# Log-sum-exp of 16,384 rows: an empty operation with a wait on VectorE, one wait for the last logarithms, and another list of loads

## The chip, the core and the metric

The kernel runs on one NeuronCore of a Trainium2 chip. The metric is the device time of one execution in microseconds (us); the median of three runs of the kernel before is 162.41 us (162.29 to 162.56). The profile is of one further execution.

## What is computed

For `x` of shape 32 x 512 x 1024 in float32, the logarithm of the sum of exponentials of each row of 1024:

```
max_x = np.max(x, axis=-1, keepdims=True)
max_x.squeeze(-1) + np.log(np.sum(np.exp(x - max_x), axis=-1))
```

The kernel takes the exponentials without subtracting the maximum, sums and takes the logarithm; at the end it tests that all sums lie in a safe range, and only if one does not, a second, slow pass with the maximum follows (it is in the program behind a branch, and isn't executed with this data).

## The kernel before

The 16,384 rows are spread over the 128 partitions, 128 rows of 1024 columns to each: 131,072 columns of a partition, 512 bytes of HBM for each column over all partitions, 67.1 MB in all. Nineteen loads (load 0 to load 18, list `LOADS`, L20) bring them into a ring of 48 rows in SBUF. The first number of an entry is the size of the load in rows; sizes are not whole rows, so a load may end inside one. They fall from 16 rows (16,384 columns) to 480 and 448 columns.

SyncE issues all loads in order (`load`, L130, the DMA itself L136). It waits only where a load overwrites a part of the ring that is still to be read: the helper `Counted.wait` puts a wait for the reader's count in front. Each load has a semaphore of its own.

ScalarE takes the exponential of each load in place, in one or several ACTIVATEs (L224), each with one wait for the load. The string of an entry says how the rows that are then whole are summed:

- `R8`: VectorE reduces eight rows in one TENSOR_REDUCE (L235).
- `G4`: GpSimd adds the right half of four rows to the left (L230), and a later `H` has VectorE reduce the halves (L154).
- `T3`: three times for one row, VectorE adds the right half to the left and sums the result into one number in the same instruction (`add_halves`, L159; L162 in the profile). The profile shows behind each a second instruction, the read of the accumulator. Such a pair is called a T below.
- `a` and `b`: the last row comes in two loads. `a` is exponentiated and summed by a shorter T (288 columns a half); `b` is summed by ScalarE itself in its ACTIVATE (L219), followed by a read of its accumulator.
- `C`: VectorE works out the least and the total of the sums found so far (L171), for the test.
- `L`: ScalarE takes the logarithms of the first 112 rows early (L197), and SyncE stores them (L255).

The last part, behind the loop over the loads, is this: ScalarE waits until VectorE has summed all rows but the last, takes 15 logarithms (L259), waits for VectorE's sum of `a` and for its own sum of `b`, and takes the last logarithm of their sum (L262). SyncE stores the 16 results (L266). Beside this VectorE tests the remaining sums (L270, L274), TensorE adds the flags up over the partitions (L279 to L282), VectorE compares (L286), ScalarE and VectorE read the flag and branch, and SyncE clears the semaphores and waits for the store.

The order on each engine is the order of the code; there is no scheduler. The waits that matter for the change: VectorE waits before the first T of each load for ScalarE's exponential of that load (`dve.wait(act, at)`); where an instruction has one such wait it carries it itself.

Of the kernel before, what the change touches and what calls it, by code (L numbers as in the profile page):

```python
# [10 lines left out]
RING = 48  # L11
B = 16

# [1 line left out]


LOADS = [  # L20
# [5 lines left out]
]  # L26


# [23 lines left out]
def kernel(  # L52
# [5 lines left out]
    nc = tc.nc  # L58
# [15 lines left out]
    H = d // 2  # L74
    W = NC - B
    LAST = NC - 1
# [36 lines left out]
    act = Counted(nc, nc.scalar, "act")  # L113
    dve = Counted(nc, nc.vector, "dve")
# [15 lines left out]
    def load(i, here, done_before, size):  # L130
        for a, b, who, at in users:
            if a < here + size and b > here:
                sp.wait(who, at)
        assert not any(p0 < here + size and p0 + s * d > here for _, p0, s, _ in folded)
        users[:] = [u for u in users if not (u[0] < here + size and u[1] > here)]
        return nc.sync.dma_start(  # L136
            out=ring[:, here : here + size], in_=source(done_before, size)
        ).then_inc(landed[i], 16)
# [7 lines left out]
    summed = []  # L146
# [3 lines left out]
    def sum_folded():  # L150
        for c0, p0, s, at in folded:
            dve.wait(pool, at)
            half = ring[:, p0 : p0 + s * d].rearrange("p (c d) -> p c d", d=d)[:, :, 0:H]
            at = dve.did(nc.vector.reduce_sum(out=sumexp[:, c0 : c0 + s], in_=half, axis=AX.X))  # L154
            users.append((p0, p0 + s * d, dve, at))
            summed.append((c0, c0 + s, at))
        folded.clear()

    def add_halves(v, col):  # L159
        h = v.shape[-1] // 2  # L160
        lo = v[:, 0:h]
        return dve.did(nc.vector.scalar_tensor_tensor(  # L162
            out=lo, in0=lo, scalar=1.0, in1=v[:, h : 2 * h],
            op0=ALU.mult, op1=ALU.add, accum_out=sumexp[:, col : col + 1],
        ))

    def check_early(c):
        dve.wait(act, summed_by_act)
        dve.wait(dve, dve.n)
        for op, col in ((ALU.min, LEAST), (ALU.add, TOTAL)):  # L170
            dve.did(nc.vector.tensor_reduce(  # L171
                out=sumexp[:, col : col + 1], in_=sumexp[:, 0:c], op=op, axis=AX.X
            ))

    for i, (size, parts) in enumerate(loads):
        if here + size > RING * d:
            assert here == p
            p = here = 0
        dma = load(i, here, done_before, size)
        first_load = first_load or dma.ins  # L180
        end = here + size
        done_before += size
        act.wait(landed[i], 16)
        for k, part in enumerate(parts):
            if part[0][0] == "H":
                sum_folded()
                continue
            if part[0][0] == "C":
                assert not folded
                checked = c  # L190
                check_early(c)
                continue
            if part[0][0] == "L":
                assert c >= W
                assert dve.seen[act.sem.num] >= summed_by_act
                act.wait(dve, max(at for c0, _, at in summed if c0 < W))
                ln_early = act.did(nc.scalar.activation(  # L197
                    out=res[:, 0:W], in_=sumexp[:, 0:W], func=AF.Ln
                ))
                continue  # L200
            if part[0][0] == "A":
                assert here == p
                for _ in range(part[0][1]):
                    v = ring[:, p : p + d]
                    summed_by_act = act.did(nc.scalar.activation(
                        out=v, in_=v, func=AF.Exp, accum_out=sumexp[:, c : c + 1]
                    ))
                    users.append((p, p + d, act, summed_by_act))
                    by_act += 1
                    c += 1  # L210
                    p += d
                    here += d
                continue
            rows = sum(s for how, s in part if how in "RTG")
            more = any(q[0][0] not in "HLC" for q in parts[k + 1 :])
            upto = p + rows * d if more else end
            v = ring[:, here:upto]
            if part[-1][0] == "b":
                last = act.did(nc.scalar.activation(  # L219
                    out=v, in_=v, func=AF.Exp, accum_out=sumexp[:, REST : REST + 1]  # L220
                ))
                here = upto
                continue
            at = act.did(nc.scalar.activation(out=v, in_=v, func=AF.Exp))  # L224
            here = upto
            for how, s in part:
                rows = ring[:, p : p + s * d].rearrange("p (c d) -> p c d", d=d)
                if how == "G":
                    pool.wait(act, at)
                    folded.append((c, p, s, pool.did(nc.gpsimd.tensor_tensor(  # L230
                        out=rows[:, :, 0:H], in0=rows[:, :, 0:H], in1=rows[:, :, H:d], op=ALU.add,
                    ))))
                elif how == "R":
                    dve.wait(act, at)
                    users.append((p, p + s * d, dve, dve.did(nc.vector.reduce_sum(  # L235
                        out=sumexp[:, c : c + s], in_=rows, axis=AX.X
                    ))))
                    summed.append((c, c + s, dve.n))
                elif how == "T":
                    dve.wait(act, at)  # L240
                    for r in range(s):
                        n_sums = add_halves(rows[:, r, :], c + r)
                        users.append((p + r * d, p + (r + 1) * d, dve, n_sums))
                        summed.append((c + r, c + r + 1, n_sums))
                elif how == "a":
                    dve.wait(act, at)
                    summed.append((LAST, NC, add_halves(ring[:, p:upto], LAST)))
                    s = 0
                c += s
                p += s * d  # L250
        assert here == end
# [3 lines left out]
    nc.sync.dma_start(out=out_rows, in_=res[:, 0:W]).then_inc(sp.sem, 16)  # L255

    sums = dve.n
    act.wait(dve, max(at for c0, _, at in summed if c0 < LAST))
    act.did(nc.scalar.activation(out=res[:, W:LAST], in_=sumexp[:, W:LAST], func=AF.Ln))  # L259
    act.wait(dve, sums)  # L260
    act.wait(act, last)
    ln_last = act.did(nc.scalar.activation(  # L262
        out=res[:, LAST:NC], in_=sumexp[:, REST : REST + 1], func=AF.Ln, bias=sumexp[:, LAST:NC]
# [10 lines left out]
    at = dve.did(nc.vector.reduce_sum(  # L274
        out=total, in_=sumexp[:, checked : TOTAL + 1], axis=AX.X
    ))
# [5 lines left out]
    at = pe.did(nc.tensor.matmul(  # L282
        count, lhsT=ones, rhs=sumexp[:, REST : REST + 1], start=False, stop=True
    ))
    dve.wait(pe, at)
    at = dve.did(nc.vector.tensor_scalar(out=fine, in0=count, scalar1=HIGH, scalar2=None, op0=ALU.is_lt))  # L286
# [111 lines left out]
```

## Time and profile before

| | us |
|---|---|
| median of three runs | 162.41 |
| profiled execution, its own time | 162.43 |
| its span, from the first to the last instruction | 161.1 |
| busy: VectorE, ScalarE, GpSimd, TensorE | 111.2, 114.7, 44.4, 0.3 |

The span is 1.3 us shorter than the time of the same execution; that part lies around the program. Times in the rows count from the start of the span. In a row of the timeline stand the start, the duration, the engine, the line, the operation, what it writes and reads, how often, and in brackets the idle time before it and who ended it. Lines `L...` are those of the kernel before.

### The profile page before, as it was taken

To read this page: it belongs to the slowest core of one execution; us is meant where nothing else is said; L and a number is where in the kernel's file an instruction comes from. 1 tells how busy PE (TensorE), PEld (TensorE's weight loads), DVE (VectorE), ACT (ScalarE), POOL (GpSimd) and SP (SyncE) were. 2 spreads that over 40 slices of the span, in tenths; PEclk is the share of its full clock that TensorE was granted. 3 is DMA by queue.
4 is the path that set the end of the run, shared out by engine and by line. 5 is a ranking of instruction groups with operands and counts; after the bars stand their busy time and mean duration, and the time that the engine had idled before them with its cause. 6 is when DMAs were issued, how large, how long until landed. Compare 5 with 4: busy or idle time off the path is not lost.

```text
span 161.1 us, 185 instructions
## 1 busy us (share of the span) xinstructions
PE 0.3 (0%) x6; PEld 0.2 (0%) x6; DVE 111.2 (69%) x57; ACT 114.7 (71%) x30; POOL 44.4 (28%) x16
## 2 busy tenths in 40 slices
PE   0000000000000000000000000000000000000000
PEld 0000000000000000000000000000000000000000
DVE  0000000009999699959997299988939999999995
ACT  3000059990899529990599719997994999999995
POOL 0000000000000000008409992005009579895000
DMA  8996996999799799969997999989899999999991
GB/s 277 505 521 277 505 511 287 479 511 411 343 498 498 343 408 504 504 268 488 485 485 318 409 432 461 485 378 469 383 479 403 394 410 443 427 412 428 417 402 30
DMA packets 3025, 67.18 MB, mean 417 GB/s; under 512 B 592, under 2 KB 848, under 8 KB 1488
## 3 DMA queue, kind: packets, MB, share of 16 engines
q1 hardware_dynamic: 3024, 67.18, 97.4%
q14 instruction: 1, 0.01, 0.0%
HBM read 67.11 MB, written 0.07 MB: 417 GB/s over the span
## 4 chain that ended last, share of the span: by engine, by line
DMA 56%; ACT 23%; DVE 13%; another core or an unknown queue 3%; SPq 2%; issue 0%; PE 0%
DMA ring<-in_x_dram 56%; ACT ring L224 23%; DVE sumexp L235 13%; SPq L136 2%; DVE ring L162 0%; DVE clamped L270 0%; PE count L279 0%; DVE fine L286 0%; DVE total L274 0%; PE count L282 0%; PE count L280 0%
## 5 line engine op out<-in xcount | busy, mean ns | idle before, releaser
L224 ACT ACTIVATE ring<-ring 128x3072 f32<-128x3072 f32 (+22 forms) x24 | 112.3, 4730 | 43.5 <-DMA ring<-in_x_dram 43.4
L235 DVE TENSOR_REDUCE sumexp<-ring 128x3 f32<-128x3072 f32 (+7 forms) x9 | 79.2, 8803 | 47.8 <-ACT ring L224 47.8
L230 POOL TENSOR_TENSOR ring<-ring 128x2048 f32<-128x2048 f32 (+4 forms) x10 | 44.1, 4420 | 101.4 <-ACT ring L224 101.4
L154 DVE TENSOR_REDUCE sumexp<-ring 128x4 f32<-128x2048 f32 (+4 forms) x10 | 22.1, 2224 | 0.1
L162 DVE SCALAR_TENSOR_TENSOR ring<-ring 128x512 f32<-128x512 f32 (+1 forms) x16 | 9.8, 671 | 0.6 <-ACT ring L224 0.4
L123 ACT ACT_TABLE_LOAD x1 | 1.3, 1283 | 1.4 <-PEq L61 1.4
L162 DVE DVE_READ_ACCUMULATOR ring<-ring 128x1 f32 x16 | 1.3, 81 | 0.0
L219 ACT ACTIVATE ring<-ring 128x448 f32<-128x448 f32 x1 | 0.6, 559 | 0.0
L279 PE MATMUL count<-far,bad 128*1 128x1 f32 x2 | 0.2, 163 | 159.6 <-DVE total L274 159.6
L286 DVE TENSOR_SCALAR fine<-count 1x1 int32<-1x1 f32 x1 | 0.1, 147 | 0.5 <-PE count L282 0.5
L171 DVE TENSOR_REDUCE sumexp<-sumexp 128x1 f32<-128x89 f32 x2 | 0.4, 240 | 0.0
L124 POOL MEMSET ones<- 128x1 f32 x1 | 0.1, 99 | 1.0 <-POOLq L61 1.0
L279 PEld LDWEIGHTS count<-far,bad 128*1 128x1 f32 x2 | 0.1, 80 | 159.6 <-issue 159.6
L262 ACT ACTIVATE res<-sumexp 128x1 f32<-128x1 f32 x1 | 0.3, 294 | 0.0
L197 ACT ACTIVATE res<-sumexp 128x112 f32<-128x112 f32 x1 | 0.3, 279 | 0.0
L270 DVE SCALAR_TENSOR_TENSOR clamped<-sumexp 128x40 f32<-128x40 f32 x1 | 0.2, 200 | 0.0
L259 ACT ACTIVATE res<-sumexp 128x15 f32<-128x15 f32 x1 | 0.2, 197 | 0.0
L274 DVE TENSOR_REDUCE total<-sumexp 128x1 f32<-128x41 f32 x1 | 0.2, 190 | 0.0
L280 PE MATMUL count<-total,ones 128*1 128x1 f32 x2 | 0.2, 163 | 0.0
L282 PE MATMUL count<-sumexp,ones 128*1 128x1 f32 x2 | 0.2, 163 | 0.0
L219 ACT ACTIVATION_READ_ACCUMULATOR ring<-ring 128x1 f32 x1 | 0.2, 186 | 0.0
L382 POOL MEMSET const-float32-0.0<- 128x1 f32 x1 | 0.1, 99 | 0.2 <-issue 0.2
(7 smaller groups left out, 0.7 us busy)
## 6 DMA issues: line engine op xcount, KB each, us to landing
ring<-in_x_dram SPq DMA_DIRECT2D x1, 8032.0 KB, 39.5
ring<-in_x_dram SPq DMA_DIRECT2D x1, 7920.0 KB, 25.0
ring<-in_x_dram SPq DMA_DIRECT2D x1, 7840.0 KB, 57.7
ring<-in_x_dram SPq DMA_DIRECT2D x1, 7632.0 KB, 25.4
ring<-in_x_dram SPq DMA_DIRECT2D x1, 5952.0 KB, 25.5
ring<-in_x_dram SPq DMA_DIRECT2D x1, 5360.0 KB, 21.2
ring<-in_x_dram SPq DMA_DIRECT2D x1, 3968.0 KB, 24.2
ring<-in_x_dram SPq DMA_DIRECT2D x1, 2448.0 KB, 20.1
```

Source lines behind the costliest of these rows:

```text
L123: nc.scalar.preload_act_table_set("natural_log_exp_and_others")
L136: return nc.sync.dma_start(out=ring[:, here : here + size], in_=source(done_before, size)).then_inc(landed[i], 16)
L154: at = dve.did(nc.vector.reduce_sum(out=sumexp[:, c0 : c0 + s], in_=half, axis=AX.X))
L162: return dve.did(nc.vector.scalar_tensor_tensor(out=lo, in0=lo, scalar=1.0, in1=v[:, h : 2 * h], op0=ALU.mult, op1=ALU.add, accum_out=sume ...
L171: dve.did(nc.vector.tensor_reduce(out=sumexp[:, col : col + 1], in_=sumexp[:, 0:c], op=op, axis=AX.X))
L197: ln_early = act.did(nc.scalar.activation(out=res[:, 0:W], in_=sumexp[:, 0:W], func=AF.Ln))
L219: last = act.did(nc.scalar.activation(out=v, in_=v, func=AF.Exp, accum_out=sumexp[:, REST : REST + 1]))
L224: at = act.did(nc.scalar.activation(out=v, in_=v, func=AF.Exp))
L230: folded.append((c, p, s, pool.did(nc.gpsimd.tensor_tensor(out=rows[:, :, 0:H], in0=rows[:, :, 0:H], in1=rows[:, :, H:d], op=ALU.add,))))
L235: users.append((p, p + s * d, dve, dve.did(nc.vector.reduce_sum(out=sumexp[:, c : c + s], in_=rows, axis=AX.X))))
L262: ln_last = act.did(nc.scalar.activation(out=res[:, LAST:NC], in_=sumexp[:, REST : REST + 1], func=AF.Ln, bias=sumexp[:, LAST:NC]))
L279: pe.did(nc.tensor.matmul(count, lhsT=bad, rhs=far, start=True, stop=False))
```

## The change

Four edits. (1) Ahead of the T of load 15, the fourth load from the end, VectorE gets an empty operation; the wait for ScalarE's exponential of load 15, which the T carried, then stands in front of the empty operation, and in the built program it is an instruction of its own that only waits. (2) The 15 logarithms now wait for VectorE's last sum, that of `a`, and no longer for the last but one; the separate wait ahead of the last logarithm is gone. (3) Nine of the nineteen loads have other sizes, as the table shows; loads 0 to 8 and load 10 keep theirs. (4) Some entries have other strings: load 2 is reduced by VectorE alone, load 4 is cut in three ACTIVATEs and is reduced by VectorE alone, load 6 has its `C` one step later, and loads 11 and 12 have two Ts each in place of three and one.

| load | 9 | 10 | 11 | 12 | 13 | 14 | 15 | 16 | 17 `a` | 18 `b` |
|---|---|---|---|---|---|---|---|---|---|---|
| columns before | 4512 | 3232 | 2496 | 1760 | 1280 | 928 | 640 | 608 | 480 | 448 |
| columns after | 4256 | 3232 | 2528 | 1696 | 1376 | 992 | 672 | 640 | 512 | 480 |

```diff
+HELD = 15
...
-    (16, "R16"), (15.6875, "R15"), (15.3125, "R11+G5 H"), (15.46875, "G7 R3+G5 H"),
-    (14.90625, "R6 H G2+R7 H"), (11.625, "R8+G4"), (10.46875, "H C G4 H R3 G3"),
-    (7.75, "H G4 R4 H"), (4.78125, "G2 H G3 H"), (4.40625, "T4"), (3.15625, "T3 L"),
-    (2.4375, "T3"), (1.71875, "T1"), (1.25, "T1"), (0.90625, "T1"), (0.625, "T1"),
-    (0.59375, "T1"), (0.46875, "a"), (0.4375, "b"),
+    (16, "R16"), (15.6875, "R15"), (15.3125, "R16"), (15.46875, "G7 R3+G5 H"),
+    (14.90625, "R4 R7 R4"), (11.625, "R8+G4"), (10.46875, "H G4 H C R3 G3"), (7.75, "H G4 R4 H"),
+    (4.78125, "G2 H G3 H"), (4.15625, "T4"), (3.15625, "T3 L"), (2.46875, "T2"), (1.65625, "T2"),
+    (1.34375, "T1"), (0.96875, "T1"), (0.65625, "T1"), (0.625, "T1"), (0.5, "a"), (0.46875, "b"),
...
                 elif how == "T":
                     dve.wait(act, at)
+                    if i == HELD:
+                        nc.vector.nop(nofuse=True)
                     for r in range(s):
...
-    act.wait(dve, max(at for c0, _, at in summed if c0 < LAST))
+    act.wait(dve, sums)
     act.did(nc.scalar.activation(out=res[:, W:LAST], in_=sumexp[:, W:LAST], func=AF.Ln))
-    act.wait(dve, sums)
     act.wait(act, last)
```

## The prediction

> **What bounds the kernel now.** I read the page's DMA part first, then the chain of waits, then the DMA view and the table by stretches at its last step, then the timeline of the last 12 us.
>
> ```profile
> DMA packets 3025, 67.18 MB, mean 417 GB/s; under 512 B 592, under 2 KB 848, under 8 KB 1488
> ...
> q1 hardware_dynamic: 3024, 67.18, 97.4%
> q14 instruction: 1, 0.01, 0.0%
> ```
>
> The DMA engines are busy 97.4% of the span: from the first load to the last the kernel moves bytes, and only what stands behind the last bytes can be saved. One packet is no load: q14, an instruction packet.
>
> ```profile
> 132.07 0.45 SPq L136
> 132.52 0.04 issue
> 132.56 25.45 DMA ring<-in_x_dram
> 158.01 0.02 issue
> 158.03 0.61 ACT ring L224
> 158.64 0.02 issue
> 158.67 0.48 DVE ring L162 x2
> ...
> 159.50 0.14 issue
> ```
>
> The chain ends with load 17 (`a`), landed at 158.01; ScalarE's exponential, VectorE's T and the test follow without a gap over 0.14. Was `a` on time? Load 16 was issued at 132.07 and has this row (304 KB, last column us to landing):
>
> ```profile
> ring<-in_x_dram SPq DMA_DIRECT2D x1, 304.0 KB, 24.7
> ```
>
> So it landed at 156.77. Here is the table by stretches (busy time of PE, PEld, DVE, ACT, POOL, then clock, DMA share, GB/s):
>
> ```profile
> 150.00:157.00 7.00, 0.00 (x0) 0.00 (x0) 6.88 (x25) 7.00 (x8) 0.00 (x0) 1.00 1.01 410
> ```
> ```profile
> 157.50:157.95 0.45, 0.00 (x0) 0.00 (x0) 0.45 (x3) 0.00 (x0) 0.00 (x0) 1.00 0.08 22
> 157.95:158.30 0.35, 0.00 (x0) 0.00 (x0) 0.28 (x2) 0.27 (x1) 0.00 (x0) 1.00 0.05 15
> 158.30:160.40 2.10, 0.29 (x6) 0.21 (x6) 0.93 (x6) 1.28 (x5) 0.00 (x0) 1.00 0.00 0
> 160.40:160.70 0.30, 0.00 (x0) 0.00 (x0) 0.00 (x0) 0.00 (x0) 0.00 (x0) 1.00 0.31 28
> ```
>
> At 410 GB/s a column (512 bytes) takes 1.25 ns: `a` (480 columns) was due at 156.77 + 0.60 = 157.37 and `b` (448) at 157.93. `a` came 0.64 late. And from 157.50 to 158.30 the share is 0.08 and 0.05, about one engine of sixteen (0.06): a single DMA engine is behind while the others have finished. The DMA view of the stretch 156.57 to 156.58 has the cause that I take:
>
> ```profile
> q14 instruction: 1, 0.01, 193.1%
> ```
>
> This packet, 193.1% of 16 x 0.01 us = 0.31 us long, sits in one engine's queue just as `a` ends and `b` begins. It fetches instructions for some engine. So the bound at the end is one DMA engine, late by 0.64.
>
> **Whose packet.** From 156 on GpSimd, TensorE and SyncE stand in waits or are done; ScalarE and VectorE advance. VectorE goes through the most instructions there, two for each T:
>
> ```profile
> 150.39 7.10 ACT L224 ACTIVATE ring<-ring 128x2496 f32<-128x2496 f32 x6
> ...
> 155.48 0.68 DVE L162 SCALAR_TENSOR_TENSOR ring<-ring 128x512 f32<-128x512 f32 x1
> ...
> 156.29 0.69 DVE L162 SCALAR_TENSOR_TENSOR ring<-ring 128x512 f32<-128x512 f32 x1
> ...
> 156.92 0.69 DVE L162 SCALAR_TENSOR_TENSOR ring<-ring 128x512 f32<-128x512 f32 x1
> ...
> 157.54 0.69 DVE L162 SCALAR_TENSOR_TENSOR ring<-ring 128x512 f32<-128x512 f32 x1
> 158.03 0.60 ACT L224 ACTIVATE ring<-ring 128x480 f32<-128x480 f32 x1 [0.55 <-DMA ring<-in_x_dram]
> ...
> 158.54 0.56 ACT L219 ACTIVATE ring<-ring 128x448 f32<-128x448 f32 x1
> 158.67 0.46 DVE L162 SCALAR_TENSOR_TENSOR ring<-ring 128x288 f32<-128x288 f32 x1 [0.44 <-ACT ring L224]
> 159.01 0.19 ACT L219 ACTIVATION_READ_ACCUMULATOR ring<-ring 128x1 f32 x1
> 159.05 0.08 DVE L162 DVE_READ_ACCUMULATOR ring<-ring 128x1 f32 x1
> 159.10 0.20 ACT L259 ACTIVATE res<-sumexp 128x15 f32<-128x15 f32 x1
> 159.17 0.20 DVE L270 SCALAR_TENSOR_TENSOR clamped<-sumexp 128x40 f32<-128x40 f32 x1
> 159.29 0.29 ACT L262 ACTIVATE res<-sumexp 128x1 f32<-128x1 f32 x1
> ...
> 159.61 0.34 SPq L266 DMA_DIRECT2D out_dram<-res  x1
> ```
>
> The Ts of loads 13 to 16 start at 155.48, 156.29, 156.92, 157.54. From request to packet there is a lag that no row gives; the nearest is the last store, issued at 159.61 with no data before 160.40: 0.8 us. Then the fetch was asked for by 155.8, while VectorE executed load 13's T. If VectorE asked, its sequencer reads ahead of the engine, and the request came from some instruction behind. Load 14's T is the next, load 15's the one after.
>
> The Trainium skill's page "Advanced Engine Details and Errata", section "Engine Queue Depths", gives VectorE a queue of eight instructions, four Ts; by it the request would come from well behind the hold. No run here shows that depth.
>
> **The change part by part.**
>
> *The empty operation.* In the built program the number of VectorE instructions up to load 15's T is the same as before (one reduction fewer, one instruction that only waits), so the fetch belongs to the same later instruction. A wait in an instruction of its own holds the sequencer. It ends with load 15's exponential, about 156.75 (below). A request from behind it then comes after 156.8, and its packet 0.8 or more later, at 157.6 or after: behind the last bytes of the loads on that engine. Queued behind the hold are the Ts of 15, 16, `a`, and the test. Its own price: a wait in an instruction costs 0.02 (158.64 in the chain), TensorE's, in an instruction of its own, 0.14 (159.50). I take 0.10, being nearer to TensorE's; both ends are hidden, as the sum shows.
>
> *Loads 2, 4, 6.* More of it falls to VectorE:
>
> ```profile
> 72.83 11.89 DVE L235 TENSOR_REDUCE sumexp<-ring 128x11 f32<-128x11264 f32 x1 [2.06 <-ACT ring L224]
> ...
> 91.74 3.35 DVE L235 TENSOR_REDUCE sumexp<-ring 128x3 f32<-128x3072 f32 x1 [4.29 <-ACT ring L224]
> ...
> 96.23 13.02 ACT L224 ACTIVATE ring<-ring 128x5664 f32<-128x5664 f32 x2 [4.52 <-DMA ring<-in_x_dram]
> 101.53 6.54 DVE L235 TENSOR_REDUCE sumexp<-ring 128x6 f32<-128x6144 f32 x1
> ...
> 120.48 8.69 DVE L235 TENSOR_REDUCE sumexp<-ring 128x8 f32<-128x8192 f32 x1 [2.45 <-ACT ring L224]
> ...
> 139.28 4.42 DVE L235 TENSOR_REDUCE sumexp<-ring 128x4 f32<-128x4096 f32 x1 [0.37 <-ACT ring L224]
> ```
>
> Sixteen rows instead of eleven at 1.08 each: load 2's reduction ends at 90.1, under the 4.29 idle before 91.74. SyncE issues load 5 behind it, at 90.1, not 84.7; load 4 keeps the DMA busy until 96.2, so 6 us of cover remain. Load 4: R4, R7, R4 = 4.42 + 7 x 1.08 + 4.42 = 16.4 from 101.53, to 118.0, ahead of the 120.48 of load 5. The later `C` only swaps 0.4 us with a reduction. Nothing. If that cover were gone, a late load would cost its delay one for one.
>
> *The sizes.* Bytes are the same, so `b` still ends at 157.93 without the late engine. From the end backwards `b` has 480 columns, `a` 512, load 16 640: `a` lands at 157.93 - 0.60 = 157.33, load 16 at 156.69. Behind load 11 stand 224 columns more than before, so it lands 0.28 earlier and ScalarE starts it at 150.11. The six ACTIVATEs of loads 11 to 16 in the row at 150.39 take 7.10 for 7712 columns; these two rows of the groups by form give the price of a column:
>
> ```profile
> L224 ACT ACTIVATE ring<-ring 128x16384 f32<-128x16384 f32 x1 | 13.9, 13857 | 19.3 <-DMA ring<-in_x_dram 19.3
> ...
> L224 ACT ACTIVATE ring<-ring 128x480 f32<-128x480 f32 x1 | 0.6, 602 | 0.5 <-DMA ring<-in_x_dram 0.5
> ```
>
> (13857 - 602)/(16384 - 480) = 0.83 ns. With 7904 columns: 7.26, the end at 157.37; as load 16 lands only at 156.69, 157.43. Load 15's ends about 156.75, ScalarE is free again at 157.34.
>
> *The tail, without the late engine.* `a`: landed 157.33, start 157.35, 0.60 + 32 x 0.83 ns = 0.63, end 157.98. `b`: starts 157.95, its read 0.47 + 0.03 later (159.01 - 158.54), ends 158.64. VectorE: load 15's T at 156.85, a T every 0.61 to 0.62 (156.92 to 157.54), load 16's at 157.46, where its exponential (157.43) has just come, so the hold's 0.10 is hidden, and 0.14 would move it 0.03. `a`'s T follows at 158.08: VectorE, not ScalarE, binds here. Against 158.67 that is 0.59 earlier; with 16 columns fewer a half its sum is there 0.45 + 0.03 later, 158.56.
>
> *One wait.* The 15 logarithms now wait for that sum, 158.56; before they started at 159.10, ahead of VectorE's read end (159.13). Alone this costs up to 0.05. The last logarithm comes 0.19 behind (159.29 - 159.10), at 158.75 and not 159.29; the store, still 0.32 behind, at 159.07. `b`'s sum (158.64) is hidden under it. The test starts 0.60 earlier and isn't last.
>
> **Sum:** 159.07 - 159.61 = -0.54. The profiled execution took 162.43, 0.02 over the median: 161.89, or **161.9**.
>
> **Rivals.**
>
> 1. *The fetch is held too briefly.* If the lag is under 0.5, the packet comes at 157.1 to 157.5, in `b` instead of `a`. `b` is then late by up to 0.64, `a` on time, the last logarithm waits for ScalarE's sum: 162.2 to 162.45, I take 162.3. The store's 0.8 speaks against it.
>
> 2. *The fetch isn't moved*: it is ScalarE's, or its instruction lies before the hold. `a` lands 0.64 late at 157.97, starts 0.04 earlier and takes 0.03 longer; the single wait takes 0.05 back: 162.45. For it: the row names no engine. Against it: VectorE need read only two Ts ahead.
>
> The Trainium skill ("Runtime: NRT & Kernel Launch", "Instruction fetch mechanics") calls the cost of such a fetch "mostly hidden"; by that rule nothing is won here, as in rival 2. The trace disagrees: 0.64 beside a 0.31 packet.
>
> 3. *Slower: the sequencer needs the block at once.* If VectorE cannot go on until the fetched instructions are there, before its queue covered this and the hold takes the cover away. A request at 156.9, 0.8 lag, 0.31 packet and it continues at 158.0 or later, 158.5 with a lag of 1.3. If the missing instruction is load 15's T or the next to it, it and load 16's T (2 x 0.61) put `a`'s T at 159.2 to 159.7, 0.55 to 1.05 behind 158.67: 163.2. It decides only if the boundary lies ahead of load 16's T; one T further it costs under 0.3. Before, Ts run on through 156.9 and 157.5 without a gap, which speaks against it weakly.
>
> The same section of that page says that a sequencer fetches the next block while it executes the current one, which speaks against rival 3; no run here shows it.
>
> **How the numbers follow.** Forecast 0.66 (its own range 161.7 to 162.1, from 0.1 in a landing and the hold's ends), rival 1 0.12, rival 2 0.13, rival 3 0.09. The range takes in the forecast and rivals 1 and 2 and leaves out rival 3: 161.65 to 162.5. A measurement of this kernel tells 0.2%, 0.33 us, from no change: faster is below 162.09, most of the forecast: 0.66; same, rivals 1 and 2: 0.24; slower 0.10.
>
> **What would show it.** Right: the q14 packet stands after 157.5 in the DMA view; `a`'s wait ends near 157.35, the 0.55 idle before it is under 0.1; Ts run from load 15 to `a` at 0.61 without a gap; the store issues near 159.07. Rival 1: q14 before 157.5, ScalarE idle ahead of `b`. Rival 2: q14 at 156.5, `a` at 158. Rival 3: VectorE idle ahead of a T behind the hold while ScalarE has finished. Wrong in the middle: ScalarE's wait for load 5 or 6 longer than before.

## The result, and the profile after

| | before | after |
|---|---|---|
| median (runs) | 162.37 us (6) | 161.66 us (6) |
| lowest to highest | 162.17 to 162.56 | 161.56 to 161.76 |
| profiled execution, its own time | 162.43 | 161.73 |
| its span | 161.1 | 160.4 |

The ratio is 0.9957, 95% interval 0.9944 to 0.9970. The kernel is 0.71 us faster; 0.54 was forecast. 161.66 lies in the whole range (161.65 to 162.5) by only 0.01, and just under the part of it that belonged to the forecast itself (161.7 to 162.1).

The page of the kernel after, the same lines as before:

```profile
DMA packets 3025, 67.18 MB, mean 419 GB/s; under 512 B 592, under 2 KB 720, under 8 KB 1488
...
q1 hardware_dynamic: 3024, 67.18, 97.8%
q14 instruction: 1, 0.01, 0.0%
```

Still one instruction packet, and the DMA engines busy from end to end. Where is the packet? The DMA view of the kernel after for 158.20 to 158.21:

```profile
q14 instruction: 1, 0.01, 225.6%
```

It is 0.36 us long and starts at 158.20; before it stood at 156.58. The table by stretches of the kernel after (columns as in the prediction, the last two are DMA share and GB/s):

```profile
157.50:157.95 0.45, 0.00 (x0) 0.00 (x0) 0.45 (x1) 0.45 (x2) 0.00 (x0) 1.00 0.02 6
157.95:158.30 0.35, 0.00 (x0) 0.00 (x0) 0.35 (x3) 0.35 (x2) 0.00 (x0) 1.00 0.06 23
```

From 157.50 on hardly a byte is left; before, one engine carried on at a share of 0.08. The 0.06 in the second row is the instruction packet by itself (0.36 us of 16 x 0.35, counted whole where it starts), which nobody waits for. So the late engine is gone. The timeline of the tail, after:

```profile
150.02 7.79 ACT L225 ACTIVATE ring<-ring 128x2528 f32<-128x2528 f32 x7
...
156.77 0.69 DVE L163 SCALAR_TENSOR_TENSOR ring<-ring 128x512 f32<-128x512 f32 x1
...
157.38 0.69 DVE L163 SCALAR_TENSOR_TENSOR ring<-ring 128x512 f32<-128x512 f32 x1
157.77 0.60 ACT L220 ACTIVATE ring<-ring 128x480 f32<-128x480 f32 x1
...
158.00 0.44 DVE L163 SCALAR_TENSOR_TENSOR ring<-ring 128x272 f32<-128x272 f32 x1
158.28 0.19 ACT L220 ACTIVATION_READ_ACCUMULATOR ring<-ring 128x1 f32 x1
158.36 0.08 DVE L163 DVE_READ_ACCUMULATOR ring<-ring 128x1 f32 x1
158.48 0.22 ACT L262 ACTIVATE res<-sumexp 128x15 f32<-128x15 f32 x1
...
158.60 0.28 ACT L264 ACTIVATE res<-sumexp 128x1 f32<-128x1 f32 x1
...
158.90 0.34 SPq L268 DMA_DIRECT2D out_dram<-res  x1
```

ScalarE goes through loads 11 to 17 in one piece (x7); the 0.55 of idle time ahead of `a` has gone. The store is issued at 158.90, before at 159.61: the 0.71 of the result. The chain that ended last, after:

```profile
147.03 1.75 DVE sumexp L155
148.78 7.94 DVE ring L163 x25
156.72 0.05 issue
156.77 1.69 DVE ring L163 x6
158.45 0.02 issue
```

VectorE now binds from 147 to 158.45 with one gap, of 0.05, at the empty operation. The last packet of a load ends at 157.44, before at 158.03, and neither ScalarE nor VectorE stands idle for it any more.

### The profile page after: what moved, and what is told of

It reads as the page before. It is cut to its first block, busy times and chain, and to the rows that moved or that the text cites. A ratio compares the mean times of both kernels' runs of the same rounds, so it can differ in the third digit from the quotient of the medians.

```text
span 160.4 us, 183 instructions
## 1 busy us (share of the span) xinstructions
PE 0.3 (0%) x6; PEld 0.2 (0%) x6; DVE 114.6 (71%) x56; ACT 114.6 (71%) x31; POOL 36.5 (23%) x14
## 4 chain that ended last, share of the span: by engine, by line
DMA 46%; DVE 27%; ACT 24%; POOL 2%; issue 0%; PE 0%
DMA ring<-in_x_dram 46%; ACT ring L225 24%; DVE sumexp L236 16%; DVE ring L163 6%; DVE sumexp L155 5%; POOL ring L231 2%; DVE clamped L272 0%; PE count L281 0%; DVE fine L288 0%; DVE total L276 0%; PE count L284 0%; PE count L282 0%
## 5 line engine op out<-in xcount | busy, mean ns | idle before, releaser
L225 ACT ACTIVATE ring<-ring 128x7168 f32<-128x7168 f32 (+21 forms) x25 | 112.2, 4546 | 42.8 <-DMA ring<-in_x_dram 42.7
L236 DVE TENSOR_REDUCE sumexp<-ring 128x4 f32<-128x4096 f32 (+5 forms) x10 | 86.7, 8682 | 44.1 <-ACT ring L225 44.1
L231 POOL TENSOR_TENSOR ring<-ring 128x2048 f32<-128x2048 f32 (+4 forms) x8 | 36.2, 4532 | 109.2 <-ACT ring L225 109.2
L155 DVE TENSOR_REDUCE sumexp<-ring 128x4 f32<-128x2048 f32 (+4 forms) x8 | 18.0, 2278 | 0.1
L220 ACT ACTIVATE ring<-ring 128x480 f32<-128x480 f32 x1 | 0.6, 602 | 0.0
```

Source lines behind the costliest of these rows:

```text
L220: last = act.did(nc.scalar.activation(out=v, in_=v, func=AF.Exp, accum_out=sumexp[:, REST : REST + 1]))
L231: folded.append((c, p, s, pool.did(nc.gpsimd.tensor_tensor(out=rows[:, :, 0:H], in0=rows[:, :, 0:H], in1=rows[:, :, H:d], op=ALU.add,))))
```

## The experiments

All were compared with the kernel before on the same chip. Each packet time is the start of q14 in the one execution that was profiled; the us are the median of several.

| run | what | us | ratio, 95% | packet | engine late at the end |
|---|---|---|---|---|---|
| e1 | after, the operation's wait met long ago | 161.62 | 0.9948 to 0.9975 | 157.50 | no |
| e2 | before, with the hold alone | 161.82 | 0.9964 to 0.9985 | 158.23 | no |
| e3 | after, with two waits at the end | 161.56 | 0.9946 to 0.9973 | 158.01 | no |
| e4 | after, no hold, 40 empty operations in front | 162.15 | 0.9982 to 1.0000 | 40.26 | yes |
| e5 | after, hold at load 13 | 161.57 | 0.9943 to 0.9973 | 157.12 | no |
| e6 | after, hold at load 16 | 161.72 | 0.9957 to 0.9977 | 158.72 | no |
| e7 | after, no hold, one operation in front | 161.57 | 0.9944 to 0.9971 | 157.17 | no |
| e8 | after, met wait and two waits | 161.67 | 0.9954 to 0.9978 | 157.79 | no |
| e9 | after, no hold, three operations in front | 162.15 | 0.9979 to 0.9996 | 155.91 | yes |
| e10 | e7 with two more GpSimd memsets | 161.57 | 0.9937 to 0.9963 | 157.12 | no |
| e11 | before, new strings of loads 2, 4, 6 | 162.30 | 0.9989 to 1.0006 | 156.53 | yes |
| e12 | before, new sizes of the last loads | 161.59 | 0.9936 to 0.9962 | 157.08 | no |

My theory was that the hold moves the packet behind the last load, and that the packet's place makes the gain. The rival was that the sizes and strings make it.

**e1, the wait taken out of the hold.**

```diff
-                    dve.wait(act, at)
                     if i == HELD:
+                        nc.vector.wait_ge(pool.sem, 1)
                         nc.vector.nop(nofuse=True)
+                    dve.wait(act, at)
```

> The changed kernel, but the empty operation ahead of load 15's T waits for a semaphore that was met at the start of the kernel; load 15's T carries its own wait again. The number of VectorE's instructions is that of the changed kernel; nothing holds its sequencer. Theory (the hold moves the instruction packet behind the loads): q14 is back at 156.3 to 156.8, one DMA engine is late, a lands near 157.8, VectorE is idle ahead of a's T, and the time is 162.1 to 162.4. Rival (the new sizes and strings made the gain): 161.6 to 161.7, wherever the packet falls.

The theory missed: 161.62, as the changed kernel, and the packet at 157.50. In the trace the operation is recorded at 155.96, although its wait was met from the start, just behind the start of load 14's T (155.94). That T carries a wait of its own, for load 14's exponential, and the operation came up only behind it. So this run had not taken away all that holds VectorE back near the end. It left both theories open, and e7 takes the operation out of the place.

**e2, the hold alone.**

```diff
                     dve.wait(act, at)
+                    if i == HELD:
+                        nc.vector.nop(nofuse=True)
```

> The kernel before with the hold alone: an empty operation with the wait ahead of load 15's T, old sizes, old strings, two waits at the end. Theory: q14 after 157.8, a lands near 157.35 and not 158.01, its T starts near 158.2 and not 158.67, and the time is 161.8 to 161.95, most of the gain. Rival (sizes and strings made it): 162.3 to 162.4. A third case (the hold makes VectorE starve): over 162.5.

161.82, inside what the theory expected: with everything else old, the hold moves the packet from 156.58 to 158.23, and the late engine goes. The store, by this timeline of e2, is issued at 158.87:

```profile
157.45 0.69 DVE L164 SCALAR_TENSOR_TENSOR ring<-ring 128x512 f32<-128x512 f32 x1
157.78 0.58 ACT L221 ACTIVATE ring<-ring 128x448 f32<-128x448 f32 x1
...
158.06 0.45 DVE L164 SCALAR_TENSOR_TENSOR ring<-ring 128x288 f32<-128x288 f32 x1
...
158.87 0.34 SPq L270 DMA_DIRECT2D out_dram<-res  x1
```

**e3, the waits at the end.**

```diff
-    act.wait(dve, sums)
+    act.wait(dve, max(at for c0, _, at in summed if c0 < LAST))
     act.did(nc.scalar.activation(out=res[:, W:LAST], in_=sumexp[:, W:LAST], func=AF.Ln))
+    act.wait(dve, sums)
     act.wait(act, last)
```

> The changed kernel with the old pair of waits at the end: the 15 logarithms wait for the last sum but one, the last logarithm for VectorE's and ScalarE's last sums. By the trace of the changed kernel VectorE's sum is there at 158.44 and ScalarE's at 158.46; a separate wait then puts the last logarithm at 158.56 at the best, not 158.60. Expected: 161.6 to 161.7, no difference that can be told. If the separate wait costs 0.1 or more as an instruction of its own: 161.75.

161.56 beside 161.66: a little under what was expected, and nothing that the intervals tell apart.

**e4, the packet early.**

```diff
+    for _ in range(40):
+        nc.vector.wait_ge(pool.sem, 1)
+        nc.vector.nop(nofuse=True)
...
-                    if i == HELD:
-                        nc.vector.nop(nofuse=True)
```

> The changed kernel without the hold, and with 40 empty operations (their wait met at the start) ahead of VectorE's first reduction, while it is idle anyway. If the packet belongs to VectorE's list, it moves with the count of its instructions: it should be issued some 20 reductions or Ts earlier, near 105 to 135. If it stays near 156.5, it is not VectorE's. Two theories for the time: all sixteen engines are always busy, so an engine that loses 0.3 to 0.6 anywhere is still behind at the end: 162.0 to 162.3; or the loss is made up on the way, since engines do not end together: 161.6 to 161.7.

Forty empty operations ahead of VectorE's list, and the packet stands at 40.26: it is VectorE's, and goes with the count of its instructions (it came further ahead than I expected). The time says what a packet in mid-kernel costs. ScalarE's timeline of e4, and then of the kernel after, where load 1 is taken up:

```profile
41.71 13.59 ACT L229 ACTIVATE ring<-ring 128x16064 f32<-128x16064 f32 x1 [5.96 <-DMA ring<-in_x_dram]
60.17 13.27 ACT L229 ACTIVATE ring<-ring 128x15680 f32<-128x15680 f32 x1 [4.88 <-DMA ring<-in_x_dram]
```
```profile
40.92 13.59 ACT L225 ACTIVATE ring<-ring 128x16064 f32<-128x16064 f32 x1 [5.09 <-DMA ring<-in_x_dram]
59.44 13.27 ACT L225 ACTIVATE ring<-ring 128x15680 f32<-128x15680 f32 x1 [4.93 <-DMA ring<-in_x_dram]
```

Load 1 is 0.79 late, load 2 0.73. And at the end of e4 one engine of sixteen is still behind:

```profile
157.50:157.95 0.45, 0.00 (x0) 0.00 (x0) 0.45 (x1) 0.45 (x2) 0.00 (x0) 1.00 0.07 26
157.95:158.30 0.35, 0.00 (x0) 0.00 (x0) 0.35 (x3) 0.35 (x2) 0.00 (x0) 1.00 0.05 16
```

What the engine lost at 40 it never made up in 117 us. The trace's records of the semaphores say the same: each load's semaphore is counted up by sixteen arrivals, and in e4 the last of the sixteen comes 0.18 behind the fifteenth for load 0, 0.86 for load 1, and 0.77 to 0.80 for every load from load 2 to `b`. In the kernel after it is never more than 0.04. 162.15 is 0.58 over the 161.57 of e7.

**e5, the hold two loads earlier, and e6, one later.** `HELD = 13` and `HELD = 16`.

> The changed kernel with the hold two loads earlier, ahead of load 13's T. In the runs so far the packet starts 1.48 to 1.54 us after the empty operation was executed, whichever its wait (156.69 to 158.20, 155.96 to 157.50, 156.76 to 158.23, 156.49 to 158.01). Here the operation can run at about 155.1. Theory (the hold sets the packet's time): q14 at 156.5 to 156.8, in the last loads, one engine late by about 0.6, time 162.1 to 162.3. Rival (any empty operation near the end helps, by something else than the packet's place): 161.6.

> The changed kernel with the hold one load later, ahead of load 16's T. Theory, if the instruction that asks for the packet lies behind load 16's T: q14 1.5 us after about 157.3, at 158.7 to 158.9, time 161.6 to 161.75 (the hold's 0.1 now stands directly ahead of the last Ts). If it lies between load 15's T and load 16's: the hold comes too late, q14 at 156.4 to 156.8, time 162.1 to 162.3.

e6 came as expected: the instruction that asks for the packet lies behind the hold at load 16 too, and the packet comes 1.44 behind the operation (157.28 to 158.72). e5 missed: the packet came at 157.12, not by 156.8, and the time is 161.57. So a hold that should have been too early to help did not hurt either, which set the question for e7: does the changed kernel need any?

**e7, no hold.**

```diff
+    nc.vector.wait_ge(pool.sem, 1)
+    nc.vector.nop(nofuse=True)
...
-                    if i == HELD:
-                        nc.vector.nop(nofuse=True)
```

The one operation in front keeps VectorE's count.

> The changed kernel with its one empty operation ahead of VectorE's first reduction instead of load 15's T, so that the count of instructions stays and nothing stands between the Ts. New sizes, strings and the one wait as changed. Theory: q14 at 156.2 to 156.8 again, a lands 0.5 to 0.8 late (near 157.8), time 162.1 to 162.3: without the packet's move the change is worth 0.0 to 0.2. Rival (sizes and strings make the gain): 161.6 to 161.7.

161.57, and the packet at 157.17, although nothing stands between the Ts. The theory that the hold makes the gain falls for the changed kernel. That the packet's place makes it still stands: in the packet records no packet of a load follows the instruction packet on its engine, which had done its part of `b` by 157.17 (the slowest engine at 157.51), and none was late.

**e8** put the edits of e1 and e3, which had looked a little faster, together; two of their lines:

```diff
+                        nc.vector.wait_ge(pool.sem, 1)
...
+    act.wait(dve, max(at for c0, _, at in summed if c0 < LAST))
```

> The empty operation with a wait met long ago, and the old pair of waits at the end, in the changed kernel: the two forms that came out at 161.62 and 161.56 together. VectorE's Ts lose nothing at the hold (load 15's T 0.07 earlier) and the last logarithm 0.03 to 0.1: expected 161.45 to 161.6, at most 0.15 under the changed kernel's 161.66; if the parts do not add up, 161.6.

161.67: the parts do not add up; e1, e3 and e8 are all the changed kernel's time.

**e9, the packet brought back.** e7 with three operations in front in place of one.

> The changed kernel without the hold, with three empty operations ahead of VectorE's first reduction where the run before had one (161.57, its packet at 157.17, behind that engine's last load). Theory (only the place of the packet matters, and it goes with the count of VectorE's instructions): two instructions more make the request one T earlier, q14 at 156.4 to 156.7, one DMA engine late at the end by 0.5 to 0.8, time 162.1 to 162.3. Rival (with the new sizes the packet does no harm wherever it falls): 161.55 to 161.7.

The packet stands at 155.91 (expected 156.4 to 156.7), and the time is 162.15, 0.58 over e7 (and over e10, measured on the same chip as e9), for two empty operations that ran before the first load had landed. The timeline of e9:

```profile
157.66 0.63 ACT L229 ACTIVATE ring<-ring 128x512 f32<-128x512 f32 x1 [0.58 <-DMA ring<-in_x_dram]
158.24 0.60 ACT L224 ACTIVATE ring<-ring 128x480 f32<-128x480 f32 x1
158.32 0.44 DVE L167 SCALAR_TENSOR_TENSOR ring<-ring 128x272 f32<-128x272 f32 x1 [0.51 <-ACT ring L229]
...
159.28 0.34 SPq L270 DMA_DIRECT2D out_dram<-res  x1
```

The 0.58 of idle time ahead of `a` is the 0.55 of the kernel before over again. So with the new sizes too it is the packet's place that decides.

**e10, e11, e12: what had moved the packet without a hold?** e10 gives GpSimd back its two instructions, e11 takes the strings alone (with one empty operation in front), e12 the sizes alone (loads 9 and 11 to 18, with the Ts of 11 and 12).

```diff
+    spare = sbuf("spare", 2)
+    pool.did(nc.gpsimd.memset(spare[:, 0:1], 0.0))
+    pool.did(nc.gpsimd.memset(spare[:, 1:2], 0.0))
```

> The changed kernel without the hold and with one empty operation in front, plus two more memsets of GpSimd at the start, so that GpSimd has as many instructions as before the change. VectorE's count to load 13's T is that of the kernel before, yet its packet came 0.6 later (157.17, not 156.58). Theory (the block's border depends on where VectorE's list lies behind the other engines' lists, and GpSimd's is two shorter since the change): q14 back at 156.4 to 156.7, time 162.1 to 162.3. Rival (GpSimd's count has nothing to do with it): q14 at 157.0 to 157.3, time 161.5 to 161.7.

> The kernel before with the strings of loads 2, 4 and 6 of the changed one, and one empty operation in front to keep VectorE's count; old sizes, two waits, no hold. GpSimd has two instructions fewer. If these strings move the packet: q14 at 157.0 to 157.3, no engine late, time 161.8 to 161.9 as with the hold alone. If they do nothing: q14 near 156.58, time 162.2 to 162.4.

> The kernel before with the new sizes of loads 9 and 11 to 18 and their Ts (two and two for loads 11 and 12); old strings, two waits, no hold. GpSimd's and VectorE's counts are those of the kernel before. Theory (the packet's place decides, and these sizes do not move it): q14 at 156.4 to 156.7, a late by 0.5 to 0.8, time 162.1 to 162.3. Rival (the sizes make the gain, or move the packet): 161.55 to 161.7.

GpSimd's count has nothing to do with it: with two instructions more the packet is at 157.12 and the time 161.57. The strings do nothing: 162.30, the packet at 156.53, here behind `a` and ahead of all of `b` on its engine, as e11's timeline shows (`a` is on time, `b` is what ScalarE waits for):

```profile
158.16 0.45 DVE L165 SCALAR_TENSOR_TENSOR ring<-ring 128x288 f32<-128x288 f32 x1
158.46 0.58 ACT L222 ACTIVATE ring<-ring 128x448 f32<-128x448 f32 x1 [0.47 <-DMA ring<-in_x_dram]
...
159.55 0.34 SPq L269 DMA_DIRECT2D out_dram<-res  x1
```

The sizes alone do everything: 161.59, the packet at 157.08 by this row of the DMA view from 157.08 to 157.09, with no hold and two waits:

```profile
q14 instruction: 1, 0.01, 193.1%
```

My theory had expected 162.1 to 162.3 for e12. It missed. The profiled execution of e12 took 161.89, the slowest of its five: there the sixteenth arrival is 0.24 to 0.29 behind the fifteenth for every load from load 0 on. That engine was behind from the start, long before the packet, and it too never caught up.

## Why the prediction came out as it did

The time came out inside the range, but the reason given for it was only in part the one that worked. The forecast rested nearly the whole gain on the hold, and the runs reach the same time without it; that the new sizes happen to move the packet too is luck.

**The late engine** was right. In the kernel before and in the three runs whose packet starts by 156.58 (e4, e9, e11), one engine is late at the end and the times are 162.15 to 162.37; in the ten kernels whose packet starts at 157.08 or later none is late by more than the 0.29 of e12, and they are 161.56 to 161.82. Nothing lies between. The 0.31 us of the packet is only about half of the delay (0.65 for `a` in the kernel before). In the packet records of the kernel before, the five packets that follow the instruction packet on its engine take 0.12 to 0.25 us each, where others of their size take 0.07; in e9 and e11 four and five packets do the same. Why they are slow isn't shown.

**Whose packet**: right, by e4.

**The hold**: right in what it does (e2: packet 1.65 later, 0.45 of time), wrong in that it was the part that counts. "So the fetch belongs to the same later instruction" held the packet to be at 156.6 in the changed kernel but for the hold. e7 and e12 show it at 157.1 to 157.2 without one, past the last load, at the full gain. So the step that failed is the one by which the packet would stay in place but for the hold: the new sizes alone move it (156.58 before, 157.08 in e12). Either the hold or the sizes move the packet past the load; together they give no more than the sizes alone. The lag, taken as 0.8 or more, is 1.44 to 1.52 from the operation to the packet with the real hold ahead of load 15 or 16 (156.69 to 158.20 in the kernel after), so rival 1 was far off. Its price was wrong as well: packets at 157.08 to 157.17 (e5, e7, e10, e12) fell behind `b` on their engine and cost nothing. Why the new sizes bring the packet 0.5 to 0.6 later at the same count of instructions is **open**: load 13's T, two Ts ahead of load 15's, starts at 155.48 before and at 155.24 in e7, so from it the lag is 1.10 and 1.93. Whether VectorE asks later, or the DMA engine serves the request later, these runs don't tell. That the packet starts within 0.09 in these four runs, while load 13's T starts anywhere from 155.24 to 155.62, points to the DMA engine, without showing it.

**The sizes** were priced only as a shift of landings, at no gain of their own. Beside moving the packet they seem to be worth some 0.2: e2, with the packet out of the way and the old sizes, is at 161.82, e12 at 161.59, and their intervals do not meet, if only just, and come from two chips. e9, which has every edit but the hold, agrees: with its packet among the loads it is still 0.18 under the kernel before on the same chip (ratio 0.9979 to 0.9996). Where the 0.2 comes from isn't shown: in the traces e2 issues its store at 158.87, the kernel after at 158.90.

**The tail**: the forecast store was at 159.07, measured 158.90. VectorE binds, as forecast, and the 0.17 lies in three terms of its path. ScalarE starts load 11 at 150.02, not 150.11, so that load 15's T, and with it `a`'s T, comes 0.08 earlier (158.00, not 158.08). The last logarithm starts 0.12 behind the fifteen, not 0.19; the 0.19 had been read off a kernel with a wait for VectorE between the two, which the change takes out. And the store follows 0.30 behind, not 0.32. `b`, taken up at 157.77 and not 157.95, is not on this path. The hold's price, 0.10, was about right (load 15's T starts at 156.77, 0.11 behind its exponential's end by the trace, where others follow within 0.04), but it was not hidden as the sum had it: load 16's T starts 0.61 behind load 15's, when load 16's exponential had ended 0.09 before. In the time this can't be told (e7 161.57, the kernel after 161.66).

**Middle part**: right. Load 2's sixteen rows stay under the idle time of VectorE, and load 4's three reductions (the row at 101.45, ending at 117.71; 118.0 was forecast) end ahead of load 5's at 120.38, by the timeline after:

```profile
72.74 17.22 DVE L236 TENSOR_REDUCE sumexp<-ring 128x16 f32<-128x16384 f32 x1 [2.05 <-ACT ring L225]
...
91.66 3.35 DVE L236 TENSOR_REDUCE sumexp<-ring 128x3 f32<-128x3072 f32 x1 [1.70 <-ACT ring L225]
...
101.45 16.26 DVE L236 TENSOR_REDUCE sumexp<-ring 128x4 f32<-128x4096 f32 x3
...
120.38 8.69 DVE L236 TENSOR_REDUCE sumexp<-ring 128x8 f32<-128x8192 f32 x1 [2.67 <-ACT ring L225]
```

**Rivals 2 and 3**: where the packet isn't moved (e11) the time is the old one, as rival 2 had it. Rival 3, VectorE stopping for its instructions, appears nowhere: in e6 the packet runs from 158.72 to 159.10, and the Ts of load 16 (157.35) and `a` (157.96) both start before it does.

## What to carry to other kernels

When the transfers bound a kernel, look for packets that aren't data: one 8 KB instruction packet among the last loads cost 0.45 us (e2 against the kernel before) to 0.58 us (e9 against e7) here. Its place hung on the count of one engine's instructions (e9 has two empty operations more, at the very start) and, at the same count, on the sizes of the last loads (e12). Here a DMA engine that fell behind stayed behind to the end (e4, from 40 us on), so no later load absorbs it; the packet has to go behind the last load. And a part that works alone (e2) is not thereby the part that works in the whole: take it out of the whole as well (e7).

## What the runs showed of the hardware that was not expected

An instruction packet of 0.31 us put one engine behind the others by 0.77 to 0.86 us at 40 us (e4; it was 0.18 for load 0, ahead of the packet) and by 0.67 to 0.69 at 156 us (e9), over twice its own length. The packets behind it on that engine were slow too: in e9 four of 2,048 bytes took 0.20 to 0.29 us each, where others of that size take 0.08. And an empty operation whose wait was met from the start was recorded only at 155.96, when the T ahead of it, which waits for ScalarE, had started at 155.94 (e1). It did not run ahead in VectorE's stream; that it holds anything back itself isn't shown.
